# Where the S5 branch keeps its inputs and outputs, and where its six gelus are made

## The chip, the cores and the metric

One core of a Trainium2 chip runs the whole program in one launch. The metric is the device time of an execution in microseconds (us); a kernel's time is the median of its runs. The engines are named as in the profile: PE is the matmul engine (PEld its weight loads), DVE the vector engine, ACT the scalar engine, POOL the GpSimd engine, and SP the engine whose queue issues the DMAs.

## What is computed

The program is one "first block" (three branches that are gated and merged) and then two layers of a "second block", on a sequence of 512 tokens with 1024 channels. The change touches the first block alone, and there the S5 branch, a diagonal state-space model on 768 channels:

```
def first_block(x, mem, ...):
    h = rms_norm(x, g_norm)
    q, k, v, fl, gf, u, gs, qm, gm, gl = split_cols(h @ w_in)
    y_fox = forgetting_attention(q, k, v, log_sigmoid(fl + b_forget)) * silu(gf)

    y_s5 = s5_ssm(u, lam_re, lam_im, log_step, b_re, b_im, c_re, c_im, d_skip)
    y_s5 = gelu(y_s5)
    y_s5 = y_s5 * sigmoid(y_s5 @ w_glu + b_glu)
    y_s5 = y_s5 * silu(gs)

    y_mem = memory_attention(qm, mk, mv) * silu(gm)
    merged = gates[0] * (y_fox @ w_proj_fox) + gates[1] * (y_s5 @ w_proj_s5) + gates[2] * (y_mem @ w_proj_mem)
    return rms_norm(x + merged @ w_out, g_final)
```

Everything is fp32. A product of fp32 matrices is made of three matmuls on split operands: high by high, low by high, high by low.

## The kernel before

**Tiles.** Data lie in SBUF as tiles of 128 partitions by 512 fp32 values, nearly all from one ring of 85 (`u()`). A projection is made in blocks: one block is 128 output channels by 512 tokens in one PSUM bank (`pmm`, three of them), so 24 matmuls of 128x512 where there are 8 tiles of input channels, and 18 where there are 6. Two or more blocks share a strip of weights. A strip is loaded (`wr`), its high part is cast on ACT (`wh`, L93), and its low part is the difference (`wl`, L96), made on DVE or POOL. Strips are split three ahead of the one in use.

**Order.** Each engine runs its own queue in the order in which a scheduler wrote it, from the program order and its own estimates, so an instruction that waits holds up all behind it on its engine. Some long work is written as generators in the background: `tick` advances them by a rate for every block of foreground work, up to each `yield`, which names a cost. The S5 generator has rate 0.2, later 0.25; the generator that makes the second block's modulation (`ada_gen`, tiles `adw` and `adacc`, L491 to L520: each round sums eight `adw` tiles into one `adacc` on DVE) has rate 0.37 and starts in `s5_out`.

**The first block in order of time.** A head projects the six tiles of u. `upost` (L1498) copies each to SBUF, writes it to a DRAM tensor `ud[j]`, and reads it back at once in another layout (`u4`, four DMAs, L1505): channels and time are interleaved differently in the scan. Then `fox` makes the forgetting attention of six pairs of heads (scores L320, exponentials L388, products with v L409 to L411), `memory` the memory attention and its projection, and `s5_out` (L1689) finishes the S5 branch. Under `fox` and `memory` the S5 generator (`s5_gen`, L1334) works through six batches, one per tile of u.

**A batch** (`s5_batch`, L1228) makes transposes (L1258), input matmuls (L1269), a scan on DVE, small matmuls (L1313) whose result DVE copies into `s5to` (L1318), and 12 matmuls (L1322 to L1324) into `py`. DVE adds the skip term (`s5du`), four DMAs write it to DRAM (`yd[j]`, L1329), and one DMA reads it back in the order of the projections (`s5y`, L1331).

**The gelu** of a batch (`gelu`, L1675) is seven instructions on one 128x512 tile: Square on ACT (L1679), a tensor_scalar (L1084) and a product (L1087) on DVE, Tanh on ACT (L1682), (t+1)*y on DVE (L1090), the high part `yh` on ACT (L1420) and the low part `yl` on DVE (L1090). In `s5_gen` the gelu of batch j-1 comes behind batch j, for j from 1 to 5, each followed by a yield of 1.5. The yields of the six batches and the five gelus make 86.1 together.

**s5_out** projects gs in six blocks (24 matmuls each; ACT Tanh L1696, then a DVE product: tile `gst`). The last gelu stands behind the fourth of them (`GE = 4`). Then come six blocks of glu, 18 matmuls each: every one sums over all six gelu tiles, three matmuls per tile. Their results go through ACT (`glt`, L1703) and DVE; then the projection `p5`, and the output.

Of the kernel before, what the change touches and what calls it, by code (L numbers as in the profile page):

```python
# [1069 lines left out]
class Blk1(Blk2):  # L1070
# [2 lines left out]
    F0 = 12  # L1073
    NF = 4
    ZM = 0.6
    GE = 4
    RS5, RS5B, RADA = 0.2, 0.25, 0.37


# [146 lines left out]
                self.tt(d[r, :, :, g, :], t[2 * i][r], t[2 * i + 1][r], op)  # L1226
        yield 1.3

    def s5_batch(self, j, U, y):


        S = self.S5
# [33 lines left out]
        for i in range(2):  # L1266
            p = self.p("a")
# [22 lines left out]
        a, b2, c, d = (self.u(name="s5h") for _ in range(4))  # L1290
# [25 lines left out]
        for i in range(4):  # L1316
            n = 128 - 32 * i
# [9 lines left out]
        self.tt(du, du, py, ALU.add)  # L1327
        for i in range(4):
            self.nc.sync.dma_start(out=self.yd[j].rearrange("(q c) (i b) -> i c q b", q=4, i=4)[i], in_=v4(du)[32 * i:32 * i + 32])  # L1329
        y[j] = self.u(name="s5y")  # L1330
        self.nc.sync.dma_start(out=y[j], in_=self.yd[j])  # L1331
        yield 0.6

    def s5_gen(self, u, y, ge, ges):  # L1334
        for j in range(6):
            yield from self.s5_batch(j, u[j], y)
            if j > 0:
                self.gelu(j - 1, ge, ges)
                yield 1.5

    def forget_load(self):
        nc = self.nc
# [131 lines left out]
    def block1(self):  # L1474
        nc, b = self.nc, self.base
        cst = self.t(b, [128, 1], F32, "hpi")
        nc.vector.memset(cst, 1.5707963267948966)
        self.halfpi = cst
        self.bmh = self.t(b, [128, 24], F32, "bmh")
        nc.vector.tensor_scalar(out=self.bmh, in0=self.col("b_merge", 0, 24), scalar1=0.5, scalar2=None, op0=ALU.mult)  # L1480
        self.bgh = self.t(b, [128, 6], F32, "bgh")
        nc.vector.tensor_scalar(out=self.bgh, in0=self.col("b_glu", 0, 6), scalar1=0.5, scalar2=None, op0=ALU.mult)
        x = [self.u(name="x") for _ in range(8)]
        with self.tc.high_priority():
            for hf in range(2):
                for j in range(8):
                    if 8 * hf + j == self.F0:
                        self.fetch(0)
                    nc.sync.dma_start(out=self.half(x[j], hf), in_=self.half(self.a["x"][:, j, :], hf))
        for hf in range(2):  # L1490
            for j in range(8):
                self.sq_acc(self.half(x[j], hf), j, slice(256 * hf, 256 * hf + 256))
        h = self.new_h()
        norm = self.norm(x, self.col("g_norm", 0, 8), None, h)
        u = [None] * 6
        self.y5 = [None] * 6

        def upost(j):  # L1498
            def f(pm):
                t = self.u(name="us")  # L1500
                nc.scalar.copy(t.rearrange("p (i b) -> p b i", i=4), pm.rearrange("p (b i) -> p b i", i=4))
                nc.sync.dma_start(out=self.ud[j], in_=t)
                u[j] = self.u(name="u4")
                for i in range(4):
                    nc.sync.dma_start(out=u[j][32 * i:32 * i + 32].rearrange("p (q b) -> p q b", q=4),  # L1505
                                      in_=self.ud[j].rearrange("(q c) (i b) -> i c q b", q=4, i=4)[i])
            return f
        self.head(["u"] * 2, h, [upost(j) for j in range(2)],
                  norm, self.half, True)
        del x, norm  # L1510
        fl = self.forget_load()
        self.s5_load()
        self.load16()
        self.merge(self.strip("u", h, 8, [upost(j) for j in range(2, 6)]), [])
        merged = []
        ge, ges = [], ([], [])
        hm = self.fox(h, u, ge, ges, merged, fl)
        self.memory(h, hm, merged)
        return self.s5_out(h, ge, ges, merged)

    def fox(self, h, u, ge, ges, merged, fl):
        nc = self.nc
        g = self.forget(h, *fl)
        next(g)
        self.lag.append(g)
        yf = [None] * 6
        Q, K, V, FK = {}, {}, {}, {}
        blks = [slice(128 * i, 128 * i + 128) for i in range(4)]

        def f_proj(p):  # L1530
            def vev(pm, b0, nb):
                for i in range(2):
                    key = p + i
                    if b0 == 0:
                        V[key] = self.v_new()
                    self.v_put(V[key], pm[:, :, 128 * i:128 * i + 128], b0, nb)

            def put(isq):
                def f(pm):
                    self.put(pm, isq, lambda hh, t: (Q if isq else K).__setitem__(2 * p + hh, t), 0.125 if isq else None)  # L1540
                    if not isq:
                        t = self.ring.tile([128, 2, T], BF16, tag="u", name=f"fk{p}", bufs=self.NU)
                        for hh in range(2):
                            nc.scalar.activation(out=t[:, hh, :], in_=self.FK, func=AF.Copy,
                                                 scale=self.self_f[:, 2 * p + hh:2 * p + hh + 1])
                            FK[2 * p + hh] = t[:, hh, :]
                return f
            it = self.tm_items("fv", h, 256, vev) if p % 2 == 0 else []
            return it + self.strip("fqk", h, 8, [put(True), put(False)])

        def f_unit(p):
            def dst(j):
                if yf[p] is None:
                    yf[p] = self.u(name="yf")
                return yf[p]
            return self.unit(
                2,
                lambda qb: [[(0, 128 * qb + 128, "f", blks[qb], slice(0, 128 * qb + 128), (128 * qb, 128, self.mcq_))]],
                lambda: [([(128 * k, T - 128 * k, "f", slice(128 * k, T), blks[k], (128 * k, 128, self.mck_))],
                          [("f", k, slice(128 * k, T))]) for k in range(4)],  # L1560
                lambda j, g: self.pairs(Q[2 * p + j], K[2 * p + j]),
                lambda j, g, kb: self.v_get(V[p], kb, j),
                dst, extra=lambda j: (self.FQ, FK[2 * p + j]))
        units = [f_unit(p) for p in range(6)]
        self.merge(f_proj(0), [])
        self.s5_setup()
        self.s5 = self.add_bg(self.s5_gen(u, self.y5, ge, ges), self.RS5)
        self.merge(f_proj(1), units[0][0])
        G = {}
        gi = self.gate_items("gf", 6, h, G)  # L1570
        yfs = [], []
        it = self.branch_items(0, "pf", 6, h, yfs, merged)
        fill = gi + it[:4]
        for p in range(6):
            if p == self.PM:
                mem = self.mem_load()
            a = units[p][1]
            if p < 5:
                a = self.mix(a, units[p + 1][0], self.ZF)
            self.merge(a, f_proj(p + 2) if p < 4 else fill[:self.NF] if p == 4 else fill[self.NF:])  # L1580
        self.gated(G, yf, yfs)
        self.s5[2] = self.RS5B
        hm, mi = self.mem_prep(*mem)
        self.merge(self.mix(it[4:], mi, self.ZM), [])
        return hm
# [100 lines left out]
        ges[0].append(hi)  # L1686
        ges[1].append(lo)

    def s5_out(self, h, ge, ges, merged):  # L1689
        nc = self.nc  # L1690
        y5, gt = ([], []), []
        self.add_bg(self.ada_gen(0), self.RADA)

# [16 lines left out]
        it = []  # L1710
        for s in range(3):
            it += self.strip("gs", h, 8, [gs, gs])
        self.merge(it[:self.GE], [])
        self.gelu(5, ge, ges)
        self.merge(it[self.GE:], [])
        for s in range(3):
            for f in self.strip("glu", ges, 6, [glu(2 * s), glu(2 * s + 1)]):
                f()
# [69 lines left out]
        h = self.new_h()  # L1788
# [268 lines left out]
```

## Time and profile before

| | |
|---|---|
| time before, median of 3 runs | 2445.68 us (2441.32 to 2447.8) |
| profiled execution, its own time | 2442.14 us |
| span of that execution | 2440.4 us |
| PE busy | 2324.2 us, 95% |
| DVE busy | 1541.2 us, 63% |
| ACT busy | 1061.3 us, 43% |
| POOL busy | 887.8 us, 36% |
| mean granted clock of PE | 0.982 of full speed |

All times within the span count from its start. The first block takes roughly the first 830 us. The six gs blocks start at 621.28 us, the last batch of S5 and the memory projection lie just ahead of them. The clock column of a stretch is the mean of what was granted in it: 1.0 is 2.4 GHz, 0.5 is 1.2 GHz.

### The profile page before, as it was taken

To read this page: it belongs to the slowest core of one execution; us is meant where nothing else is said; L and a number is where in the kernel's file an instruction comes from. 1 tells how busy PE (TensorE), PEld (TensorE's weight loads), DVE (VectorE), ACT (ScalarE), POOL (GpSimd) and SP (SyncE) were. 2 spreads that over 40 slices of the span, in tenths; PEclk is the share of its full clock that TensorE was granted. 3 is DMA by queue.
4 is the path that set the end of the run, shared out by engine and by line. 5 is a ranking of instruction groups with operands and counts; after the bars stand their busy time and mean duration, and the time that the engine had idled before them with its cause. 6 is when DMAs were issued, how large, how long until landed. Compare 5 with 4: busy or idle time off the path is not lost.

```text
span 2440.4 us, 33141 instructions
## 1 busy us (share of the span) xinstructions
PE 2324.2 (95%) x12138; PEld 1938.6 (79%) x12138; DVE 1541.2 (63%) x2573; ACT 1061.3 (43%) x1995; POOL 887.8 (36%) x810
## 2 busy tenths in 40 slices
PE   6989989998999889999999999999999999999999
PEld 5877768876878867787888888887778788888888
DVE  7566887666899798658368684257974846422222
ACT  4355544443333435653444324343565444523432
POOL 2445446545232274236123223125531623122212
PEclk9999999999999999999999999999999999999999
DMA  4311122312676331122136563242211324223222
GB/s 154 110 44 52 57 76 93 113 52 66 227 269 236 124 97 53 52 79 86 61 122 246 207 237 112 82 136 76 69 48 54 98 74 139 70 95 113 95 87 87
DMA packets 105619, 265.35 MB, mean 109 GB/s; under 512 B 13664, under 2 KB 23408, under 8 KB 105456
## 3 DMA queue, kind: packets, MB, share of 16 engines
q1 hardware_dynamic: 104304, 261.47, 31.7%
q8 instruction: 95, 1.56, 0.3%
q10 hardware_dynamic: 1152, 1.77, 0.2%
q14 instruction: 68, 0.56, 0.1%
HBM read 244.69 MB, written 9.44 MB: 104 GB/s over the span
## 4 chain that ended last, share of the span: by engine, by line
PE 67%; DVE 9%; issue 4%; POOL 3%; ACT 2%; DMA 1%; SPq 0%; POOLq 0%; DVEq 0%; ACTq 0%
PE pmm L117 18%; PE pmm L119 18%; PE pmm L118 18%; PE ps L320 3%; DVE wl L96 1%; DVE adacc L514 1%; PE ppv L409 1%; PE ppv L411 1%; PE ppv L410 1%; DVE l L232 1%; POOL qv L632 1%; PE pmm L134 1%; PE pmm L135 1%; PE ps L629 1%; PE pmm L133 1%
## 5 line engine op out<-in xcount | busy, mean ns | idle before, releaser
L96 POOL TENSOR_TENSOR wl<-wr,wh 128x512 fp32r<-128x512 f32 x346 | 482.4, 1413 | 1149.2 <-ACT wh L93 945.0
L117 PE MATMUL pmm<-h,wh 128*128 128x512 f32 (+1 forms) x2112 | 826.0, 392 | 6.5 <-ACT wh L93 2.8
L119 PE MATMUL pmm<-h,wl 128*128 128x512 f32 (+1 forms) x2112 | 825.8, 392 | 4.5 <-POOL wl L96 4.3
L118 PE MATMUL pmm<-l,wh 128*128 128x512 f32 (+1 forms) x2112 | 823.6, 390 | 0.0
L117 PEld LDWEIGHTS pmm<-h,wh 128*128 128x128 f32 x2112 | 400.6, 190 | 86.9 <-ACT wh L93 3.8
L119 PEld LDWEIGHTS pmm<-h,wl 128*128 128x128 f32 x2112 | 400.4, 190 | 86.4 <-POOL wl L96 7.0
L118 PEld LDWEIGHTS pmm<-l,wh 128*128 128x128 f32 x2112 | 400.7, 190 | 77.7 <-DVE l L230 0.4
L93 ACT CAST wh<-wr 128x512 fp32r<-128x512 f32 (+1 forms) x692 | 385.7, 611 | 135.7 <-DMA wr<-in_w 102.2
L96 DVE TENSOR_TENSOR wl<-wr,wh 128x512 fp32r<-128x512 f32 x346 | 288.4, 863 | 27.9 <-ACT wh L93 24.0
L392 DVE TENSOR_TENSOR pl<-pe,ph 128x512 fp32r<-128x512 f32 (+4 forms) x168 | 111.9, 674 | 133.9 <-ACT ph L390 131.9
L230 DVE TENSOR_TENSOR l<-r,h 128x512 fp32r<-128x512 f32 x64 | 46.4, 725 | 220.8 <-ACT h L222 216.7
L972 DVE SCALAR_TENSOR_TENSOR x<-pmm,ada,x 128x512 f32<-128x512 f32 (+1 forms) x88 | 59.9, 682 | 179.8 <-PE pmm L119 179.4
L514 DVE SCALAR_TENSOR_TENSOR adacc<-adw,cact,adacc 128x512 f32<-128x512 f32 x168 | 156.5, 933 | 3.2
L320 PE MATMUL ps<-qk,qk 128*128 128x512 f32 (+4 forms) x416 | 140.5, 363 | 11.2 <-DVE unm L345 3.6
L995 ACT ACTIVATE r<-pmm 128x512 f32<-128x512 f32 x62 | 37.1, 598 | 257.2 <-PE pmm L119 254.7
L388 ACT ACTIVATE pe<-ps 128x512 f32<-128x512 f32 (+4 forms) x168 | 84.5, 503 | 91.3 <-PE ps L320 88.8
L320 PEld LDWEIGHTS ps<-qk,qk 128*128 128x128 f32 x416 | 79.9, 193 | 32.2 <-DVE unm L345 8.0
L117 PE MATMUL pmm<-yh,wh 128*128 128x512 f32 (+1 forms) x244 | 91.1, 376 | 5.6 <-ACT yh L1420 3.6
L632 POOL TENSOR_TENSOR qv<-qv,mhalf 128x8 f32<-128x8 f32 x34 | 60.4, 1778 | 91.0 <-DVE qv L631 86.7
L119 PE MATMUL pmm<-yh,wl 128*128 128x512 f32 (+1 forms) x244 | 90.7, 373 | 1.7 <-DVE wl L96 0.9
L390 ACT CAST ph<-pe 128x512 fp32r<-128x512 f32 (+4 forms) x168 | 88.8, 529 | 7.9 <-DVE pl L392 1.7
L118 PE MATMUL pmm<-yl,wh 128*128 128x512 f32 (+1 forms) x244 | 90.5, 372 | 0.4 <-DVE yl L1090 0.4
(386 smaller groups left out, 3992.7 us busy)
## 6 DMA issues: line engine op xcount, KB each, us to landing
wr<-in_w SPq DMA_DIRECT2D x324, 512.0 KB
adw<-in_wada SPq DMA_DIRECT2D x192, 256.0 KB
xs<-xg SPq DMA_DIRECT2D x136, 64.0 KB
wr<-in_w SPq DMA_DIRECT2D x22, 384.0 KB
xd<-x SPq DMA_DIRECT2D x16, 256.0 KB
x<-xd SPq DMA_DIRECT2D x16, 256.0 KB
x<-in_x SPq DMA_DIRECT2D x16, 128.0 KB
x<-in_x SPq DMA_DIRECT2D x8, 256.0 KB
```

Of the source, the lines that this page charges most:

```text
L93: ins = self.nc.scalar.copy(h[:, 0:m], r[:, c:c + m])
L96: eng.tensor_tensor(out=l[:, 0:m], in0=r[:, c:c + m], in1=f32(h)[:, 0:m], op=ALU.subtract)
L117: mm(out, wh, ah, start=start, stop=False)
L118: mm(out, wh, al, start=False, stop=False)
L119: self.pe = mm(out, wl, ah, start=False, stop=stop).ins.name
L320: mm(outs[i] if len(r.shape) == 2 else outs[i].rearrange("p (r i) -> p r i", r=r.shape[1]), w, r, start=first and i == 0, stop=last and i ...
L388: nc.scalar.activation(out=e[:, w], in_=pt[:, w], func=AF.Exp)
L390: nc.scalar.copy(ph[:, w], e[:, w])
L392: nc.vector.tensor_tensor(out=pl[:, w], in0=e[:, w], in1=f32(ph)[:, w], op=ALU.subtract)
L514: nc.vector.scalar_tensor_tensor(out=acc, in0=w, scalar=cc, in1=acc, op0=ALU.mult, op1=ALU.add)
L632: nc.gpsimd.tensor_tensor(out=v, in0=v, in1=self.mhalf, op=ALU.pow)
L972: nc.vector.scalar_tensor_tensor(out=x[j][:, s], in0=pm[:, s], scalar=ada[:, c + j:c + j + 1], in1=x[j][:, s], op0=ALU.mult, op1=ALU.add)
```

## The change

What it does:

- `upost` writes `ud[j]` and no longer reads it back. `s5_gen` does that: it loads batch 0 at its start, and batch j+1 just ahead of batch j's work. The same 24 DMAs now stand in SP's queue among the weight loads of the S5 stage.
- `s5_batch` writes `yd[j]` and no longer reads it back. `s5_out` issues all six reads at its start, ahead of the first `adw` loads.
- The five gelus and their yields of 1.5 leave `s5_gen`. The S5 generator is advanced at the same rates, with 78.6 of work where it had 86.1.
- `s5_out` makes all six gelus, one behind each gs block (`merge` of six blocks with six gelus). Before, five were long done and one stood behind the fourth block.

```
-        y[j] = self.u(name="s5y")
-        self.nc.sync.dma_start(out=y[j], in_=self.yd[j])
         yield 0.6
 
-    def s5_gen(self, u, y, ge, ges):
+    def s5_gen(self):
+        def load(j):
+            u = self.u(name="u4")
+            for i in range(4):
+                self.nc.sync.dma_start(out=u[32 * i:32 * i + 32].rearrange("p (q b) -> p q b", q=4),
+                                       in_=self.ud[j].rearrange("(q c) (i b) -> i c q b", q=4, i=4)[i])
+            return u
+        u = load(0)
         for j in range(6):
-            yield from self.s5_batch(j, u[j], y)
-            if j > 0:
-                self.gelu(j - 1, ge, ges)
-                yield 1.5
+            n = load(j + 1) if j < 5 else None
+            yield from self.s5_batch(j, u)
+            u = n
...
                 nc.sync.dma_start(out=self.ud[j], in_=t)
-                u[j] = self.u(name="u4")
-                for i in range(4):
-                    nc.sync.dma_start(out=u[j][32 * i:32 * i + 32].rearrange("p (q b) -> p q b", q=4),
-                                      in_=self.ud[j].rearrange("(q c) (i b) -> i c q b", q=4, i=4)[i])
...
-    def s5_out(self, h, ge, ges, merged):
+    def s5_out(self, h, merged):
         nc = self.nc
+        ge, ges = [], ([], [])
+        self.y5 = [self.u(name="s5y") for _ in range(6)]
+        for j in range(6):
+            nc.sync.dma_start(out=self.y5[j], in_=self.yd[j])
         y5, gt = ([], []), []
         self.add_bg(self.ada_gen(0), self.RADA)
...
-        self.merge(it[:self.GE], [])
-        self.gelu(5, ge, ges)
-        self.merge(it[self.GE:], [])
+        self.merge(it, [lambda j=j: self.gelu(j, ge, ges) for j in range(6)])
```

No engine gains or loses work by it but for a few scheduling rows. In the changed program the lines from L1330 on are shifted by a few, so a gelu reads L1675, L1083, L1086, L1678, L1089 and L1423 there. What the change moves is seen in the queues at three places.

**ACT in the gs stage.** `gst` is the Tanh of a gs block, `gw` the work tile of a gelu, `yh` its high part, `wh` the casts of a strip of weights. Before, from the third `gst` to the fifth:

```order
L1696 ACTIVATE gst_6206<-pmm_6181 128x512
L93 CAST wh_6220<-wr_6065 128x512
L93 CAST wh_6224<-wr_6065 128x512
L1696 ACTIVATE gst_6255<-pmm_6230 128x512
L1679 ACTIVATE gw_6267<-s5y_5876 128x512
L1682 ACTIVATE gw_6267<-gw_6267 128x512
L1420 ACTIVATE yh_6273<-gw_6267 128x512
L93 CAST wh_6277<-wr_6132 128x512
L93 CAST wh_6281<-wr_6132 128x256
L1696 ACTIVATE gst_6312<-pmm_6287 128x512
```

and now, from the third `gst` to the casts behind the fourth:

```order
L1696 ACTIVATE gst_6176<-pmm_6151 128x512
L1675 ACTIVATE gw_6190<-s5y_5997 128x512
L1678 ACTIVATE gw_6190<-gw_6190 128x512
L1423 ACTIVATE yh_6196<-gw_6190 128x512
L93 CAST wh_6200<-wr_6015 128x512
L93 CAST wh_6204<-wr_6015 128x512
L1696 ACTIVATE gst_6235<-pmm_6210 128x512
L1675 ACTIVATE gw_6247<-s5y_5998 128x512
L1678 ACTIVATE gw_6247<-gw_6247 128x512
L1423 ACTIVATE yh_6253<-gw_6247 128x512
L93 CAST wh_6257<-wr_6092 128x512
L93 CAST wh_6261<-wr_6092 128x256
```

The same six rows stand there six times over: each block's `gst` now has the whole gelu of the block ahead of it, and two casts, in front of it.

**DVE in the gs stage.** Of each gs block DVE makes the product `gst`; the rest is `adacc` sums, low parts of weights and gelu. Before, the rows about the second `gst`:

```order
L514 SCALAR_TENSOR_TENSOR adacc_6111<-adw_6103,cact_84,adacc_6111 128x512
L1090 SCALAR_TENSOR_TENSOR gst_6159<-gst_6159,pmm_6134 128x512
L514 SCALAR_TENSOR_TENSOR adacc_6111<-adw_6105,cact_84,adacc_6111 128x512
L96 TENSOR_TENSOR wl_6172<-wr_6025,wh_6171 128x512
L96 TENSOR_TENSOR wl_6176<-wr_6025,wh_6175 128x512
L514 SCALAR_TENSOR_TENSOR adacc_6111<-adw_6107,cact_84,adacc_6111 128x512
```

and now, from the end of the first gelu to the head of the third:

```order
L1089 SCALAR_TENSOR_TENSOR yl_6081<-gw_6074,yh_6080 128x512
L518 TENSOR_TENSOR adacc_6061<-adacc_6061 64x512
L1089 SCALAR_TENSOR_TENSOR gst_6119<-gst_6119,pmm_6094 128x512
L1083 TENSOR_SCALAR gw_6131<-gw_6131 128x512
L1086 TENSOR_TENSOR gw_6131<-gw_6131,s5y_5996 128x512
L1089 SCALAR_TENSOR_TENSOR gw_6131<-gw_6131,s5y_5996 128x512
L1089 SCALAR_TENSOR_TENSOR yl_6138<-gw_6131,yh_6137 128x512
L96 TENSOR_TENSOR wl_6142<-wr_5963,wh_6141 128x512
L96 TENSOR_TENSOR wl_6146<-wr_5963,wh_6145 128x512
L512 TENSOR_SCALAR adacc_6183<-adw_6062,cact_84 128x512
L1089 SCALAR_TENSOR_TENSOR gst_6176<-gst_6176,pmm_6151 128x512
```

Gelus 0, 2 and 4 have `adacc` sums between their steps, gelus 1, 3 and 5 have none. From the first `gst` to the last gelu's `yl` DVE now has 6 `gst`, 28 rows of the modulation, 4 low parts of weights and 6 gelus; before, from the first `gst` to the first glu block's product, it had 6, 26, 6 and 1.

**PE at the end of the last S5 batch.** Before, 27 matmuls of a gate projection stood between the last L1313 of batch 5 and the 12 matmuls that need `s5to`; the last three of them, and what follows:

```order
L117 MATMUL pmm_5950<-h_182,wh_5831 128x512
L118 MATMUL pmm_5950<-l_190,wh_5831 128x512
L119 MATMUL pmm_5950<-h_182,wl_5832 128x512
L1322 MATMUL ps_5856<-u_144_628,s5to_5825 128x128
L1323 MATMUL ps_5856<-s5m_5533,s5cw_5757 128x128
L1324 MATMUL ps_5856<-s5m_5535,s5cw_5758 128x128
```

and now the L1313 (L1312 in its lines) are directly ahead:

```order
L1312 MATMUL ps_5587<-s5cw_5477,s5b_1261_5581 32x128
L1312 MATMUL ps_5587<-s5cw_5478,s5b_1261_5581 32x128
L1321 MATMUL ps_5602<-u_962_4294,s5to_5596 128x128
L1322 MATMUL ps_5602<-s5m_5241,s5cw_5477 128x128
L1323 MATMUL ps_5602<-s5m_5243,s5cw_5478 128x128
```

Batch 5 itself has moved up by about 150 of PE's rows, out of the memory projection into the memory attention. At the end of `fox` it is the other way round: batch 1's L1313 and L1322 stood there with nothing between them, and now have 23 matmuls of scores, of a gate projection and of products with v in between; DVE's reciprocal for the last pair of heads (L439) stood ahead of that batch's `s5to` copies, and now stands behind them. From the first gs block on PE's queue is the same in both, but for a few neighbours swapped far behind.

## Rows read from the trace of the kernel before

**Rows 1.** The page, part 1: busy us of each engine, share, instructions.

```profile
PE 2324.2 (95%) x12138; PEld 1938.6 (79%) x12138; DVE 1541.2 (63%) x2573; ACT 1061.3 (43%) x1995; POOL 887.8 (36%) x810
```

**Rows 2.** Windows: length, busy PE, PEld, DVE, ACT, POOL; PE clock, DMA, GB/s.

```profile
100.00:621.40 521.40, 479.74 (x2582) 392.48 (x2581) 372.07 (x591) 242.65 (x466) 273.12 (x279) 0.96 0.22 72
270.00:300.00 30.00, 26.48 (x124) 20.10 (x123) 24.82 (x39) 16.55 (x31) 16.25 (x17) 0.89 0.17 52
340.00:370.00 30.00, 21.86 (x108) 18.45 (x107) 21.57 (x32) 10.52 (x19) 8.77 (x10) 0.83 0.21 66
627.55:661.80 34.25, 34.25 (x157) 28.46 (x156) 32.07 (x42) 11.37 (x21) 7.61 (x6) 1.00 0.68 235
661.80:700.00 38.20, 36.53 (x162) 29.13 (x161) 33.23 (x48) 15.70 (x30) 11.00 (x8) 1.00 0.63 217
```

**Rows 3.** Waits of PE from 100 to 621.4: total us, times, longest.

```profile
PE ps L1322 <- DVE s5to L1318: 6.0, 2, 4.7
PE ps L1313 <- DVE s5b L1309: 5.5, 3, 3.0
...
PE pmm L117 <- ACT yh L1420: 3.6, 2, 2.3
...
PE ps L320 <- ACT pe L388: 3.1, 3, 2.2
```

**Rows 4.** Timeline of PE: the first gs matmul, the first that needs gelu 5.

```profile
621.28 0.39 PE L117 MATMUL pmm<-h,wh 128*128 128x512 f32 x1
...
658.03 0.39 PE L117 MATMUL pmm<-yh,wh 128*128 128x512 f32 x1
```

**Rows 5.** Timeline of ACT: the first gs block's Tanh and two casts behind it.

```profile
626.92 0.60 ACT L1696 ACTIVATE gst<-pmm 128x512 f32<-128x512 f32 x1 [8.24 <-PE pmm L119]
627.41 1.14 ACT L93 CAST wh<-wr 128x512 fp32r<-128x512 f32 x2
```

**Rows 6.** Timeline of DVE: the first gs product, the first glu product.

```profile
627.55 0.69 DVE L1090 SCALAR_TENSOR_TENSOR gst<-gst,pmm 128x512 f32<-128x512 f32 x1 [4.66 <-ACT gst L1696]
...
661.81 0.68 DVE L1090 SCALAR_TENSOR_TENSOR gw<-glt,gw 128x512 f32<-128x512 f32 x1
```

**Rows 7.** Groups of DVE from 627.55 to 661.8: count, busy us, mean ns.

```profile
L514 DVE SCALAR_TENSOR_TENSOR adacc<-adw,cact,adacc 128x512 f32<-128x512 f32 x20 | 16.3, 813 | 0.5
...
L96 DVE TENSOR_TENSOR wl<-wr,wh 128x512 fp32r<-128x512 f32 (+1 forms) x6 | 3.3, 594 | 0.0
```

**Rows 8.** The gelu's tile: ns min/median/max of each step, first and last start.

```profile
L1679 ACT ACTIVATE gw<-s5y x6: 1085/1129/1151, 270.9 to 643.8; 128x512 f32<-128x512 f32 x6
L1084 DVE TENSOR_SCALAR gw<-gw x6: 416/418/427, 276.0 to 646.6; 128x512 f32<-128x512 f32 x6
L1087 DVE TENSOR_TENSOR gw<-gw,s5y x6: 1039/1082/1100, 276.4 to 647.6; 128x512 f32<-128x512 f32 x6
L1682 ACT ACTIVATE gw<-gw x6: 630/631/632, 277.5 to 648.7; 128x512 f32<-128x512 f32 x6
L1090 DVE SCALAR_TENSOR_TENSOR gw<-gw,s5y x6: 1036/1079/1101, 278.1 to 650.2; 128x512 f32<-128x512 f32 x6
L1420 ACT ACTIVATE yh<-gw x6: 629/632/633, 279.2 to 651.4; 128x512 fp32r<-128x512 f32 x6
L1090 DVE SCALAR_TENSOR_TENSOR yl<-gw,yh x6: 691/692/693, 279.9 to 652.0; 128x512 fp32r<-128x512 f32 x6
```

**Rows 9.** Timeline from 638 to 650 us: POOL, and two DVE sums of one form.

```profile
638.98 2.72 POOL L96 TENSOR_TENSOR wl<-wr,wh 128x512 fp32r<-128x512 f32 x2 [8.16 <-ACT wh L93]
...
640.59 1.66 DVE L518 TENSOR_TENSOR adacc<-adacc 64x512 f32<-64x512 f32 x1
...
649.37 0.69 DVE L520 TENSOR_TENSOR adacc<-adacc 64x512 f32<-64x512 f32 x1
```

**Rows 10.** Timeline about 280 us: an exponential of fox behind gelu 0.

```profile
279.22 0.63 ACT L1420 ACTIVATE yh<-gw 128x512 fp32r<-128x512 f32 x1 [1.10 <-DVE gw L1090]
279.87 0.60 ACT L388 ACTIVATE pe<-ps 128x512 f32<-128x512 f32 x1
```

More of the change, by code (lines that the diff above doesn't have):

```diff
@@ L1075 @@
     ZM = 0.6
-    GE = 4
     RS5, RS5B, RADA = 0.2, 0.25, 0.37
@@ L1227, in s5_mul, with s5_batch @@
         yield 1.3
-    def s5_batch(self, j, U, y):
+    def s5_batch(self, j, U):
         S = self.S5
@@ L1494, in block1 @@
         norm = self.norm(x, self.col("g_norm", 0, 8), None, h)
-        u = [None] * 6
-        self.y5 = [None] * 6
         def upost(j):
@@ L1515, in block1, with fox @@
         merged = []
-        ge, ges = [], ([], [])
-        hm = self.fox(h, u, ge, ges, merged, fl)
+        hm = self.fox(h, merged, fl)
         self.memory(h, hm, merged)
-        return self.s5_out(h, ge, ges, merged)
-    def fox(self, h, u, ge, ges, merged, fl):
+        return self.s5_out(h, merged)
+    def fox(self, h, merged, fl):
         nc = self.nc
@@ L1566, in fox @@
         self.s5_setup()
-        self.s5 = self.add_bg(self.s5_gen(u, self.y5, ge, ges), self.RS5)
+        self.s5 = self.add_bg(self.s5_gen(), self.RS5)
         self.merge(f_proj(1), units[0][0])
```

## The prediction

> **What bounds the kernel now.** The page's busy line comes first: PE is busy for 2324.2 us, 95% of the span, and no other engine for more than 63% [rows 1]. So the time is PE's work plus the time in which PE stands or runs at half clock, and an edit that leaves PE's matmuls alone can only change the second part. That average hides that stages have different limits, so windows come next. The S5 stage (100 to 621.4) is 521.40 us with 479.74 us of PE: 41.7 us are lost there, at a mean clock of 0.96. The stage where the gelus go is another case: from 627.55 to 661.80 PE is busy all 34.25 us, but DVE is busy for 32.07 of them, ACT for only 11.37 and POOL for 7.61 [rows 2]. DVE has 2.2 us to spare there. PE does not wait for DVE only because nothing that PE wants early stands at the end of DVE's queue.
>
> The waits tell what PE lost in the S5 stage, and the timelines where the edges of the gs stage lie; both are used below.
>
> **The edits that cost nothing by themselves.** The 24 reads of u move in SP's queue from the head of the kernel to a batch ahead of their use; the six gelus start from 270.9 to 643.8 [rows 8], so a batch lasts some 75 us, and that covers them. The six reads of `s5y` stand ahead of the `adw` loads; the first gelu cannot start before the first gs block is through ACT, 626.92 + 0.60, which is 5.6 us after that stage's first matmul [rows 4, 5]. That covers them, and if it did not, the delay would fall on the gelus priced next. The reads of batch 5 come late only if its writes do, and that batch now ends earlier than before.
>
> **The gs stage.** Five gelus are added. One costs DVE 0.418 + 1.082 + 1.079 + 0.692 = 3.27 us and ACT 1.129 + 0.631 + 0.632 = 2.39 us [rows 8]. I take the new queues row by row, from the `gst` of block 0, which starts on DVE at 627.55 as before [rows 6].
>
> DVE's content: 5 x 3.27 = 16.4 us more; two rows of the modulation more, one of them like L518's 1.66 and one of 0.81 [rows 7, 9], 2.5; two low parts of weights fewer at 0.59 [rows 7], -1.2. Against before's 34.25 us that is 34.25 + 17.7 = 52.0, less the 2.2 us that stood idle, 49.8. But not all of it can be dense. Gelus 1, 3 and 5 have no other work between their steps, and DVE waits there for Square, Tanh and `yh` on ACT: after such a `gst` 1.1 us for Square, part of it hidden, 0.63 + 0.05 for Tanh, and the same for `yh`. I take 1.3 us each, 3.9 in all: 53.7. So `yl` of gelu 5 ends near 627.55 + 53.7 = 681.2, and its `yh` 0.7 earlier, at 680.5.
>
> PE reaches the first matmul that needs gelu 5 at 658.03, 36.75 us after its first gs matmul at 621.28 [rows 4]. It is in the first of the six glu blocks, so no later glu work can go ahead of it on PE's queue. PE stands for 680.5 - 658.0 = 22.5 us, in two or three pieces (gelus 3, 4 and 5 each come later than PE wants them). The gs blocks themselves are hardly held: ACT now takes a `gst` only behind the gelu ahead of it, some 9 us apart where PE makes a block in 5.44 us, but three banks of `pmm` let PE run ahead, and what it waits there it would wait later.
>
> After a wait PE runs at half clock for a time. In the window from 270 to 300, with its waits about 280, the clock's mean is 0.89, so 30 x 0.11 = 3.3 us of full speed are missing; from 340 to 370 it is 0.83, 5.1 us for two pieces [rows 2]. One such piece after the last wait adds 3.3; pieces between the waits cost nothing, as PE is early there. Sum of the stage: +25.8.
>
> Bounds. Lower: the serial chain alone, with DVE always free. Per block ACT has `gst` 0.60, Square 1.13, then ts 0.42 and product 1.08 on DVE, Tanh 0.63, product 1.08, `yh` 0.63, and two casts 1.14 [rows 5, 8]: 6.7 us against PE's 5.44. Five times 6.7 from 626.92, then 5.57 for the last one, ends at 666.0, 8 us after 658.0; with 3.3 for the clock, +11. That would need the 28 modulation sums out of the gelus' way, and the queue puts ten to fourteen of them between steps, so I take the value near the DVE sum. Upper: each of the three pairs without cover costs 2.5 us instead of 1.3, +3.6, and the odd `adacc` waits for its load, +2: +31.
>
> One row shows a longer cost: L518, a sum of 64x512 in SBUF, took 1.66 us, most of it while POOL was at work from 638.98 to 641.70, and the same form at L520 took 0.69 [rows 9]. So an instruction of POOL can cost one of DVE's about 1.0 us. POOL has six low parts in the stage [rows 2], so up to +5.8, if each met a gelu step where it met none before. The six gelus' own steps spread little, from 1.036 to 1.101 us for the longest [rows 8], so I leave it out of the sum and keep it for the upper end. The Trainium skill (page "SBUF — State Buffer", section "Who interferes with whom") states that a DVE instruction with two SBUF inputs contends with a GpSimd instruction that reads SBUF, and that the loser blocks for the whole instruction. By that rule three of a gelu's four DVE steps can be blocked and the stage would be some +32 instead of +26; the trace agrees in L518's 1.66 us, and no gelu step in it shows it.
>
> **The S5 stage.** PE's waits that a gelu or an S5 step ends are L1322 6.0, L1313 5.5, `yh` 3.6, `pe` 3.1: 18.2 us [rows 3]. Only some of them go:
> - About 280, an exponential of fox stands on ACT behind gelu 0's `yh`, which ends at 279.85 [rows 10]; PE waits 2.2 us for it. With the gelu gone that wait goes, about 1 us of the one ahead of it, and the half-clock piece behind, 3.3 [rows 2]: -6.
> - At the end of fox PE waits 4.7 us for `s5to` (with no matmuls in between) and 2.3 for the `yh` that stood behind gelu 1 [rows 3]. Now 23 matmuls lie between L1313 and L1322, and no gelu stands ahead of `yh`. The chain from the last pair of heads remains, so I take 5 of the 7, and one of the two half-clock pieces there at 2.5: -7.
> - The last batch had its longest L1313 wait, 3.0 us [rows 3], in the memory projection. In its new place, inside the memory attention, nothing stands between L1313 and L1322; the nearest row for that is the 4.7 at the end of fox, which had a reciprocal ahead of the copies that is not there now. I take the whole 4.7 as new, with 3.3 for the clock, and the old 3.0 as gone: +5.
> - Batches 3 and 4 also move, in a stage where ACT and DVE are needed for exponentials. Nothing in the trace prices that. Bounds: all of the 18.2 and three pieces of clock vanish, about -28 for the whole stage; or the eleven us of L1322 and L1313 come twice with nothing saved, about +11. I take 0, between them.
>
> Sum: -8, from -28 to +11.
>
> **After the gs stage.** Behind the stall each engine's queue goes on as before, and the modulation is as far as it was. From 661.80 to 700 PE is busy for 36.53 of 38.20 us [rows 2], so at most 1.7 us can be made up. The second block is unchanged.
>
> **The sum.** 2442.1 + 25.8 - 8 - 1 = 2459 against the profiled execution; the median of the runs lies 3.5 above it, so about 2462.
>
> **The rivals** (2446 is the 2442.1 and the 3.5 of the sum).
> - *Faster, the S5 stage pays for all.* The 18.2 us of waits and the clock behind them vanish (-28), and the gelus cost only their serial chain (+11): 2446 - 17 = 2429. For it: these waits do name S5 steps, and one gelu in the gs stage costs PE nothing today. Against it: it needs DVE free for gelus in a stretch where it has 2.2 us of 34.25. It decides where the stage's cost falls under what the S5 stage gives back.
> - *No difference.* The gs stage is at +16, because modulation sums wait for the gelus' steps anyway and fill them, and the S5 stage gives back 16: 2446.
> - *Dearer.* Gelu steps on DVE are held up by POOL's low parts as L518 was (+32 for the stage), and the moved batches stall the memory attention for as much as they give back elsewhere (0): 2446 + 32 - 1 = 2477; with the S5 stage at its upper end of +11, 2488. For it speaks L518's row, against it the gelus' even durations. It decides where POOL works at the same time as a gelu's steps; it has the sign of the forecast.
> - *The change does not act.* The scheduler would have to leave the gelus where they were; the new queues show that it has not. No chance.
>
> **How the numbers follow.** A measurement of this kernel tells a difference from none above about 0.3%, 7.3 us. My forecast (stage +20 to +31, S5 stage -14 to 0) has 0.52, the dearer rival 0.16, no difference 0.21, faster 0.11. So slower 0.68, same 0.21, faster 0.11. The forecast's own span is about 2452 to 2477. Eight times in ten takes it from the middle of the cases without difference to the dearer rival's lower case: 2441 to 2479.
>
> **What would show it.** In the profile after: PE standing for about 22 us between the first glu block's matmuls, near 20 us of it on `yh` or `yl` of gelus 3 to 5, at granted clocks near 0.5 right after; DVE nearly full from the first `gst` to that `yl`, some 53 us where it was 34; no wait for `pe` behind a gelu about 280; `s5to` waits moved from the end of fox to the memory attention. It would be wrong if DVE shows idle time in the gs stage while PE runs through the glu blocks, or if the S5 stage as a whole changes by more than 15 us.

## The result

The changed kernel takes 2456.80 us (median of 4 runs, 2455.66 to 2458.56), the kernel before 2445.12 us beside it. The ratio is 1.0053, with a 95% interval of 1.004 to 1.0065: 11.7 us or half a per cent slower. 2462 was predicted, in a range of 2441 to 2479.

The page of the changed kernel: PE is as busy as before, and the span is longer [rows 1].

```profile
PE 2327.1 (95%) x12111; PEld 1940.2 (79%) x12138; DVE 1546.5 (63%) x2573; ACT 1061.8 (43%) x1995; POOL 886.5 (36%) x810
```

The two edges of the gs and glu stage are the Tanhs on ACT, first and last start of `gst` and `glt`:

```profile
L1696 ACT ACTIVATE gst<-pmm x6: 587/588/598, 620.3 to 664.9; 128x512 f32<-128x512 f32 x6
L1703 ACT ACTIVATE glt<-pmm,bgh x6: 678/682/689, 675.0 to 700.2; 128x512 f32<-128x512 f32 x6
```

Before, the same view gave:

```profile
L1696 ACT ACTIVATE gst<-pmm x6: 592/598/600, 626.9 to 654.1; 128x512 f32<-128x512 f32 x6
L1703 ACT ACTIVATE glt<-pmm,bgh x6: 678/682/688, 658.9 to 687.1; 128x512 f32<-128x512 f32 x6
```

So the S5 stage ends 6.6 us earlier (626.9 to 620.3), and from the first `gst` to the last `glt` it is 79.9 us where it was 60.2: 19.7 us lost. The sum is +13.1 at the last `glt`, and the first exponential of the second block (L388) comes 13.6 us later than before (946.0 against 932.4). The medians differ by 11.7. The profiled execution itself is 16.4 longer (2458.56 against 2442.14): some 3 us more lie in the second block, whose code is the same; their cause is open.

Windows of the changed kernel (columns as in [rows 2]): the S5 stage, the two windows of [rows 2] in it, and the stretch from the first `gst` product to the last gelu's `yl`.

```profile
100.00:614.60 514.60, 474.04 (x2573) 390.09 (x2581) 357.48 (x572) 231.92 (x451) 268.29 (x279) 0.97 0.24 76
...
620.90:673.90 53.00, 41.63 (x159) 31.02 (x158) 48.01 (x63) 21.60 (x35) 8.56 (x6) 0.90 0.42 145
...
270.00:300.00 30.00, 26.92 (x147) 21.13 (x147) 23.85 (x32) 18.49 (x33) 21.41 (x21) 0.94 0.23 70
340.00:370.00 30.00, 28.06 (x155) 23.51 (x154) 19.09 (x27) 13.16 (x27) 18.85 (x23) 1.00 0.27 81
```

In the 53.00 us DVE is busy for 48.01 and PE for 41.63 at a clock of 0.90; before, PE had no gap in the 34.25 us of that stretch [rows 2]. PE's timeline has the gaps one by one, in brackets:

```profile
614.63 0.39 PE L117 MATMUL pmm<-h,wh 128*128 128x512 f32 x1
...
646.56 0.50 PE L117 MATMUL pmm<-h,wh 128*128 128x512 f32 x1 [2.52 <-ACT wh L93]
...
664.24 1.14 PE L117 MATMUL pmm<-yh,wh 128*128 128x512 f32 x2 [4.60 <-DVE adacc L514]
665.18 0.63 PE L118 MATMUL pmm<-yl,wh 128*128 128x512 f32 x1
666.73 0.79 PE L118 MATMUL pmm<-yl,wh 128*128 128x512 f32 x1 [0.92 <-DVE yl L1089]
...
671.91 0.40 PE L117 MATMUL pmm<-yh,wh 128*128 128x512 f32 x1
...
673.25 1.01 PE L117 MATMUL pmm<-yh,wh 128*128 128x512 f32 x3 [0.48 <-ACT yh L1423]
```

and ACT's has what three of them waited for, the cast of a weight behind gelu 2 and `yh` of gelus 4 and 5:

```profile
645.37 0.63 ACT L1423 ACTIVATE yh<-gw 128x512 fp32r<-128x512 f32 x1 [1.76 <-DVE gw L1089]
645.90 1.12 ACT L93 CAST wh<-wr 128x512 fp32r<-128x512 f32 x2
...
663.56 0.63 ACT L1423 ACTIVATE yh<-gw 128x512 fp32r<-128x512 f32 x1 [1.76 <-DMA adw<-in_wada]
...
672.57 0.63 ACT L1423 ACTIVATE yh<-gw 128x512 fp32r<-128x512 f32 x1 [1.15 <-DVE gw L1089]
```

The 4.60 is put down to `adacc`, but the matmul reads `yh` of gelu 4, which ACT made at 663.56 for 0.63 us. The matmul of 673.25 is the one that needs gelu 5; by the distance of before (36.75 us behind the first gs matmul, [rows 4]) PE wanted it at 651.4, so it is 21.9 us late. PE's gaps up to there sum to 11.1 us: 6.0 on gelus 4 and 5 (the last three brackets), and 5.1 in and just behind the gs blocks on parts of weights, whose casts now stand behind the gelus on ACT. The rest of the 21.9 us is work. PE's matmuls started 0.43 us apart from 664.75 to 671.58, at half clock, and 0.23 apart at full clock, and the 0.48 shows that PE had work nearly until gelu 5 came. That work is the second glu block. PE's queue of the changed kernel, from the first row that reads gelu 4:

```
L117 MATMUL pmm_6386<-yh_6315,wh_6261 128x512
L117 MATMUL pmm_6429<-yh_6080,wh_6319 128x512
L118 MATMUL pmm_6429<-yl_6081,wh_6319 128x512
L118 MATMUL pmm_6386<-yl_6316,wh_6261 128x512
L119 MATMUL pmm_6386<-yh_6315,wl_6262 128x512
L119 MATMUL pmm_6429<-yh_6080,wl_6320 128x512
L117 MATMUL pmm_6429<-yh_6137,wh_6319 128x512
```

6386 is the first glu block and 6429 the second: 15 of its 18 matmuls stand ahead of the first block's rows for gelu 5. Before, all 18 rows of the first block stood ahead of the second. The text ahead of the prediction says that PE's queue is the same from the first gs block on; that is wrong at this place.

### The profile page after: what moved, and what is told of

Its sections match the earlier page's. It is cut to its first block, busy times and chain, and to the rows that moved or that the text cites. A ratio compares the mean times of both kernels' runs of the same rounds, so it can differ in the third digit from the quotient of the medians.

```text
span 2456.7 us, 33106 instructions
## 1 busy us (share of the span) xinstructions
PE 2327.1 (95%) x12111; PEld 1940.2 (79%) x12138; DVE 1546.5 (63%) x2573; ACT 1061.8 (43%) x1995; POOL 886.5 (36%) x810
## 3 DMA queue, kind: packets, MB, share of 16 engines
q10 hardware_dynamic: 1152, 1.77, 0.2%
## 4 chain that ended last, share of the span: by engine, by line
PE 63%; DVE 11%; issue 4%; POOL 3%; ACT 3%; DMA 2%; SPq 1%; POOLq 0%; DVEq 0%; ACTq 0%
PE pmm L117 17%; PE pmm L119 17%; PE pmm L118 16%; PE ps L320 4%; DVE adacc L514 1%; PE ppv L409 1%; PE ppv L411 1%; PE ppv L410 1%; DVE wl L96 1%; DMA xs<-xg 1%; POOL qv L632 1%; POOL wl L96 1%; DVE yl L1089 1%; DVE l L232 1%; DMA adw<-in_wada 1%
## 5 line engine op out<-in xcount | busy, mean ns | idle before, releaser
L118 PEld LDWEIGHTS pmm<-l,wh 128*128 128x128 f32 x2112 | 400.9, 190 | 78.6 <-DVE l L230 0.4
L96 DVE TENSOR_TENSOR wl<-wr,wh 128x512 fp32r<-128x512 f32 x346 | 282.8, 845 | 50.1 <-ACT wh L93 45.6
L388 ACT ACTIVATE pe<-ps 128x512 f32<-128x512 f32 (+4 forms) x168 | 84.5, 503 | 105.6 <-PE ps L320 102.9
L117 PE MATMUL pmm<-yh,wh 128*128 128x512 f32 (+1 forms) x244 | 91.3, 380 | 11.1 <-DVE adacc L514 4.6
```

What stands on the lines that cost most here:

```text
L96: eng.tensor_tensor(out=l[:, 0:m], in0=r[:, c:c + m], in1=f32(h)[:, 0:m], op=ALU.subtract)
L117: mm(out, wh, ah, start=start, stop=False)
L118: mm(out, wh, al, start=False, stop=False)
L388: nc.scalar.activation(out=e[:, w], in_=pt[:, w], func=AF.Exp)
```

## Experiments

The table has each kernel's median, the median of before beside it, the ratio with its interval, and the two edges. The last column is the gs and glu stage. In e4 and e11 the first `gst` stands behind a gelu on ACT, so it is no edge there.

| kernel | us | before | ratio | first gst | last glt | stage |
|---|---|---|---|---|---|---|
| before | 2445.12 | | | 626.9 | 687.1 | 60.2 |
| changed | 2456.80 | 2445.12 | 1.0053 [1.0040, 1.0065] | 620.3 | 700.2 | 79.9 |
| e1 gelus alone | 2471.78 | 2441.91 | 1.0124 [1.0109, 1.0139] | 633.7 | 713.5 | 79.8 |
| e2 DRAM alone | 2443.24 | 2441.91 | 1.0006 [0.9997, 1.0015] | 622.7 | 682.9 | 60.2 |
| e5 yields kept | 2455.92 | 2441.91 | 1.0056 [1.0041, 1.0071] | 617.5 | 697.1 | 79.6 |
| e6 no gelu arithmetic | 2435.49 | 2441.91 | 0.9973 [0.9963, 0.9982] | 618.7 | 679.2 | 60.5 |
| e3 modulation later | 2466.23 | 2443.01 | 1.0097 [1.0082, 1.0112] | 621.7 | 689.6 | 67.9 |
| e4 gelus in memory's projection | 2440.41 | 2443.01 | 0.9992 [0.9982, 1.0001] | | 680.7 | |
| e9 three gelus | 2462.92 | 2443.01 | 1.0080 [1.0063, 1.0096] | 637.2 | 703.4 | 66.2 |
| e7 e1 + u ahead | 2484.96 | 2443.01 | 1.0171 [1.0151, 1.0191] | 643.9 | 723.7 | 79.8 |
| e8 e1 + y late | 2449.02 | 2443.25 | 1.0026 [1.0015, 1.0037] | 616.3 | 696.3 | 80.0 |
| e10 y one batch later | 2473.07 | 2443.25 | 1.0121 [1.0101, 1.0141] | 635.1 | 714.3 | 79.2 |
| e11 e4 + u at once | 2434.63 | 2443.25 | 0.9961 [0.9947, 0.9975] | | 673.5 | |
| e12 ring of 79 | 2464.17 | 2444.01 | 1.0082 [1.0053, 1.0112] | 619.1 | 699.2 | 80.1 |

### The two halves of the change, and the gelu itself: e1, e2, e6

e1 is the kernel before with

```
-            if j > 0:
-                self.gelu(j - 1, ge, ges)
-                yield 1.5
...
-        self.merge(it[:self.GE], [])
-        self.gelu(5, ge, ges)
-        self.merge(it[self.GE:], [])
+        self.merge(it, [lambda j=j: self.gelu(j, ge, ges) for j in range(6)])
```

> The kernel before with the gelus alone moved behind the gs blocks; u is read back at once and y right behind its writes, as before. Theory (the loss lies in the gelus' place in the gs stage, the DRAM part is free): as the changed kernel, 2457 us within 3, first gs matmul at 614 to 616 us, first glt 60 us behind it. Rival (late reads of u or y are part of the loss): under 2452 us.

e2 is the kernel before with the other half:

```
-                u[j] = self.u(name="u4")
...
-        y[j] = self.u(name="s5y")
-        self.nc.sync.dma_start(out=y[j], in_=self.yd[j])
         yield 0.6
...
+            n = load(j + 1) if j < 5 else None
+            if j > 0:
+                self.yload(j - 1)
             yield from self.s5_batch(j, t, y)
```

> The kernel before with the DRAM part alone: u read one batch ahead, y read one batch later, gelus and their yields where they were. Theory: no difference from before, 2445 us within 4. Rival (the reads cost, behind weight loads in SP's queue): 2450 us or more.

e6 is the changed kernel with the first seven lines of `gelu`, its arithmetic, left out:

```
-        nc.scalar.activation(out=w3, in_=y, func=AF.Square)
...
-        self.stt(w3, w3, 1.0, y, ALU.add, ALU.mult)
+        w = self.y5[j]
```

> The changed kernel with the gelu's arithmetic left out: of each gelu only yh and yl remain, made from y itself, so ACT loses 1.76 us and DVE 2.58 us per gelu. Theory (the chain of the gelus through ACT and DVE is the loss): the stall before the first glu block falls under 3 us, the S5 stage keeps its 6.7 us, 2437 to 2440 us. Rival (the loss is the wait for the reads of y, or the order of ACT's queue as such): 2450 us or more.

The stage column answers one question at once: 79.8 with the gelus moved and nothing else, 60.2 with the DRAM half alone, 60.5 with the moved gelus' arithmetic left out. The 19.7 us are the moved gelus' steps in that stage, wholly: in e6 PE waits there for 1.5 us in all, for parts of weights alone, so the reads of y and the places of `yh` and `yl` on the queues cost nothing by themselves. e6 takes 2435.49 us, a little under the expected range. e2 as a whole cannot be told from before, as expected. But e1 missed by 15 us: its stage is as expected, and its S5 stage ends 13.4 us later than the changed kernel's. So with late gelus the DRAM half is not free there; it gains. That was against the theory, and e7, e8, e10 and e12 go into it below.

### What sets the end of gelu 5: e9, e3

e9 makes three gelus behind their batches again (their y is read at the start of the next batch):

```
             yield from self.s5_batch(j, u)
             u = n
+            if 0 < j < 4:
+                self.gelu(j - 1, *self.gg)
...
-        self.merge(it, [lambda j=j: self.gelu(j, ge, ges) for j in range(6)])
+        self.merge(it, [lambda j=j: self.gelu(j, ge, ges) for j in range(3, 6)])
```

> The changed kernel with gelus 0 to 2 made behind their batches again and gelus 3 to 5 in the gs stage, behind every second block. Theory (each gelu adds its 3.27 us to a DVE that has 2 us to spare): DVE's way from the first gst to the last gelu's yl is 53 - 3 x 3.3 = 43 us or a little less, PE loses 8 to 11 us before the second glu block, where it lost 20. Rival (what costs is that the last gelu stands behind the sixth block, however many there are): PE loses 18 us or more, as with six.

Its window from the first `gst` product to the last gelu's `yl` (columns as in [rows 2]), and PE's one large wait in the glu blocks:

```profile
637.90:676.80 38.90, 35.74 (x159) 29.01 (x157) 37.38 (x51) 15.06 (x26) 7.98 (x6) 0.98 0.53 183
```

```profile
675.30 1.41 PE L117 MATMUL pmm<-yh,wh 128*128 128x512 f32 x3 [3.16 <-DVE adacc L514]
```

38.90 us with three gelus, 53.00 with six: 4.7 us for each, 3.5 of them DVE's work (37.38 and 48.01 us busy) and 1.2 its waits, which stand between the steps of gelus 1, 3 and 5 of the changed kernel. The stage loses 66.2 - 60.2 = 6.0 us where six lose 19.7. The rival falls: in e9, too, the last gelu stands behind the sixth block. The expected 43 us and 8 to 11 us of loss were too much; a gelu costs more than its DVE steps. As a whole e9 takes 2462.92 us, more than the changed kernel, since its S5 stage ends at 637.2; that belongs to the next part.

e3 takes the modulation out from between the gelus:

```
-        self.add_bg(self.ada_gen(0), self.RADA)
...
         self.merge(it, [lambda j=j: self.gelu(j, ge, ges) for j in range(6)])
+        self.add_bg(self.ada_gen(0), self.RADA)
```

> The changed kernel with the modulation's generator started behind the gs blocks and not ahead of them, so that no adacc sum stands between the gelus. Theory (DVE's content, gelus plus modulation, sets when gelu 5 is done): only the serial chain through ACT and DVE remains, so the first glt comes 40 to 43 us after the first gst on ACT (54.7 in the changed kernel), PE loses about 8 us there and not 20; but the 28 sums, 22 us, must then lie behind, where DVE is 92% busy, so the whole is 2448 to 2458 us. Rival (the lockstep on ACT alone sets it): first glt still 52 to 55 us behind the first gst.

The first `glt` comes 41.0 us behind the first `gst` (662.7 and 621.7), so the chain alone is what is left, and the stage loses 7.7 us where the lower bound of the prediction had 8 before the clock. The sums on DVE between the gelus make the other 12. Up to 3 of these may be POOL's: without the sums none of the six `yl` meets POOL's work, and each takes 0.69 us, where three took 1.8 in the changed kernel. But the sums do not vanish. PE's waits of e3 from 690 to 880 us (us in total, times, longest), and the window 780 to 860 of e3 and then of before:

```profile
PE pmm L119 <- DVE wl L96: 6.1, 1, 6.1
PE ps L491 <- DVE adacc L520: 5.2, 1, 5.2
```

```profile
780.00:860.00 80.00, 58.70 (x361) 53.72 (x360) 63.78 (x115) 26.63 (x55) 17.18 (x12) 0.85 0.50 175
```

```profile
780.00:860.00 80.00, 67.18 (x459) 60.88 (x457) 66.94 (x120) 30.87 (x62) 23.61 (x17) 0.97 0.38 128
```

PE stands at the end of the block instead, for a low part of a weight that DVE made behind sums, and for the modulation itself, at a clock of 0.85, and the whole is 2466: 8 us above the expected upper end, since the sums come all at the one place where the norm needs them.

### The S5 stage: e7, e8, e10, e5, e12

e7 and e8 complete a square with e1 and the changed kernel, all four with late gelus:

| first gst | y read behind its writes | y read at the end |
|---|---|---|
| u read back at once | 633.7 (e1) | 616.3 (e8) |
| u read one batch ahead | 643.9 (e7) | 620.3 (changed) |

```
+            n = load(j + 1) if j < 5 else None
             yield from self.s5_batch(j, t, y)
```

> As e1 (gelus alone moved), with u read one batch ahead in addition; y is still read behind its writes. e1 was at 2472 us, the changed kernel at 2457; e1's first gst on ACT stood at 633.7 us, that of the changed kernel at 620.3. Theory A (the place of u's reads makes the 13 us between them): first gst at 619 to 623 us, 2456 to 2460 us. Theory B (the late read of y makes them): first gst at 631 us or later, 2468 us or more.

```
-        y[j] = self.u(name="s5y")
-        self.nc.sync.dma_start(out=y[j], in_=self.yd[j])
         yield 0.6
...
+        self.y5 = [self.u(name="s5y") for _ in range(6)]
+        for j in range(6):
+            nc.sync.dma_start(out=self.y5[j], in_=self.yd[j])
```

> As e1 (gelus alone moved), with the six reads of y moved to the end of the S5 stage in addition; u is read back at once. It fills the square of u at once or ahead and y at once or late, with late gelus: e1 had its first gst at 633.7 us, e7 at 643.9, the changed kernel at 620.3. Theory (the read of y behind its writes is what costs e1 and e7 their time, and the early reads of u cost nothing): first gst at 612 to 621 us, 2450 to 2458 us. Rival (only both together help): first gst at 630 us or later, 2466 us or more.

e7 (2484.96 us) comes as its theory B, e8 (2449.02 us) as its theory. The late reads of y give back 17.4 or 23.6 us; reading u one batch ahead costs 10.2 or 4.0. The cost of u has a place. The changed kernel's PE at 117 us:

```profile
117.16 0.61 PE L277 MATMUL ps<-c,mcm 128*128 128x128 bf16 x4 [4.22 <-DVE mcm L271]
```

and that of before:

```profile
116.08 0.40 PE L277 MATMUL ps<-c,mcm 128*128 128x128 bf16 x4
```

It waits for the last of DVE's steps there, in the changed kernel and in that of before:

```profile
116.13 0.97 DVE L271 CAST mcm<-sp 128x16 bf16<-128x16 f32 x1
```

```profile
115.06 0.57 DVE L271 CAST mcm<-sp 128x16 bf16<-128x16 f32 x1
```

That result comes 1.5 us later now, and that is the smaller part. Before, PE makes 29 more matmuls of a projection while it is on its way; with u read ahead L277 stands in front of them, and PE waits for 4.2 us, and its clock is 0.67 from 117 to 125 us, where it was 1.00. Fox's first exponential comes 7 to 8 us later than before in the changed kernel, e2, e7 and e10, which read u ahead, and 0.3 or less in e1 and e8.

For y, two causes could be meant: SP's queue stands at the read until the writes have landed, or the tiles lie in the ring. e10 has the tiles but not the stand:

```
+            if j > 0:
+                self.yload(j - 1)
             yield from self.s5_batch(j, u)
...
```

> The changed kernel with the read of y of batch j not at the end but at the start of the next batch, so SP does not stand for its writes to land, but the tiles of y lie in the ring as early as in e7. Theory A (SP's queue standing between the writes and the read costs e7 its 23 us): first gst at 618 to 624 us, 2454 to 2461 us. Theory B (the tiles held in the ring cost it): first gst at 638 us or later, 2474 us or more. Theory C (neither; each small edit throws the scheduler's order of the S5 stage another way): anything between.

e12 has six tiles fewer, and nothing else:

```
-    NU = 85
+    NU = 79
```

> The changed kernel with 79 tiles in the ring and not 85, as if six tiles were held all through; PE's queue is the same row for row. Theory (early reads of y cost their time by the order of the queues, not by the tiles that they hold): first gst at 618 to 623 us, 2455 to 2461 us, as the changed kernel. Rival (held tiles delay the loads of weights, as e10 seemed to allow): first gst at 628 us or later, 2465 us or more.

e10 stays at 635.1, between its theories A and B, and e12 at 619.1: neither the stand alone (643.9 to 635.1 by taking it away, not to 620) nor the held tiles. (e12 loses its 7 us against the changed kernel behind the last `glt`, which is at 699.2; PE's queue is the same in both through the first block, but in the second, where the ring is smaller too, it is not.) What e1, e7 and e10 share, and the changed kernel and e8 have not, is an order. DVE's timeline at the end of `fox` in e10, and PE's wait for it:

```profile
363.95 3.35 DVE L439 RECIPROCAL rs<-rs 128x512 f32<-128x512 f32 x1
367.22 0.10 DVE L208 TENSOR_SCALAR nv<-ps 128x2 f32<-128x2 f32 x1
```

```profile
PE ps L197 <- POOL nr L210: 5.4, 1, 5.4
```

and DVE in the changed kernel, where PE does not wait for `nr`:

```profile
365.29 0.15 DVE L208 TENSOR_SCALAR nv<-ps 128x2 f32<-128x2 f32 x1
365.36 3.34 DVE L439 RECIPROCAL rs<-rs 128x512 f32<-128x512 f32 x1
```

A 0.1 us step stands behind a 3.3 us reciprocal, and PE behind both. e9, which reads three of the six y early, has this order too, with a wait of 5.8 us. So early reads of y go with this order in all four kernels that have them with late gelus. That it comes from the reads is argued from these four and not shown: no run changes the order alone, and the 5.4 us are one of several places that make the 14.8 between e10 and the changed kernel. That part of the cause is open.

e5 keeps the yields, so the S5 batches stand on PE's queue where they stood before:

```
             u = n
+            if j > 0:
+                yield 1.5
```

> The changed kernel with the yield of 1.5 behind each batch kept, so that the S5 batches stand on PE's queue where they stood before, but without gelus between. Theory A (the 6.7 us that the S5 stage gave back come from the gelus being gone from ACT and DVE): first gs matmul at 614 to 617 us, 2457 us. Theory B (they come from the batches' new places): first gs matmul at 619 to 622 us, 2461 to 2464 us.

Its first `gst` is at 617.5, so theory B falls: 2.8 us ahead of the changed kernel's, and it was 3.7 us ahead at L277 already, so the batches' new places give 1 us at most. e5 and e2 differ in the gelus, and in when y is read: 617.5 against 622.7, and 3 of these 5 us arise ahead of 60 us, where the two have the same edits. That leaves 2 us or so for the gelus' absence where y is read late. Where y is read early it is the other way: e1 and before, and e10 and e2, differ in the gelus and their yields alone, and the first `gst` comes 6.8 us (633.7 against 626.9) and 12.4 us (635.1 against 622.7) later without the gelus. So the runs show no gain of the gelus' absence apart from the order that comes with it.

### A place where the gelus are hidden: e4, e11

```
-        self.merge(it[4:], [])
         self.drain(self.s5)
...
+        for j in range(6):
+            nc.sync.dma_start(out=self.y5[j], in_=self.yd[j])
+        self.merge(it[4:], [lambda j=j: self.gelu(j, self.ge, self.ges) for j in range(6)])
```

> The changed kernel with the six reads of y and the six gelus moved one stage forward, between the last 12 blocks of the memory projection, behind a drain of the S5 generator. DVE is busy there for 13.8 of 34.6 us in the changed kernel. Theory (a gelu costs nothing where DVE has room for its 3.27 us): the gs and glu stage is as in the kernel before (60 us from the first gst to the last glt), what the S5 stage gave back stays, 2435 to 2441 us. Rival (gelus between projection blocks delay PE wherever they stand, by ACT's and DVE's order): 2447 us or more.

The end of the memory projection, e4 from 580 to 612 and the changed kernel from 580 to 614.6:

```profile
580.00:612.00 32.00, 32.00 (x143) 26.50 (x142) 24.25 (x31) 17.34 (x27) 8.54 (x6) 1.00 0.24 83
```

```profile
580.00:614.60 34.60, 34.60 (x154) 28.67 (x153) 13.80 (x21) 9.99 (x18) 8.14 (x6) 1.00 0.39 134
```

DVE goes from 13.80 to 24.25 us, ACT from 9.99 to 17.34, and PE has no gap in either. The same six gelus that cost 19.7 us one stage further on cost 3 us or less here (e4's last `glt` is at 680.7; that of e6, which leaves the gelus' arithmetic out, is at 679.2). e4 is 16 us faster than the changed kernel and cannot be told from before. e11 is e4 with u read back at once:

> e4 (gelus between the blocks of the memory projection, 2440 us) with u read back at once as in the kernel before, so that the new wait of 4.2 us at 117 us is gone. If the S5 stage otherwise stays as in e4: 2432 to 2437 us, faster than before by more than the uncertainty. If its order is thrown another way: 2440 us or more.

2434.63 us, 8.6 us faster than before and 22 faster than the changed kernel: the wait at 117 us is gone, and the gelus are hidden.

## Why the prediction was right, and where not

The direction and its main mechanism held: the gelus' chain through DVE in the gs stage. The numbers step by step:

- **DVE's way through the stage**: 53.7 us predicted, 53.00 measured. That it is so close is in part luck, as two parts of it missed and cancel. Three `yl` took 1.8 us and not 0.69, each while POOL made low parts: +3.3. The three L512 took 0.48 and not about 1.4, since POOL did not work beside them: -2.9. DVE in the changed kernel (POOL's 3.03 us run from 646.58):

```profile
621.50 0.48 DVE L512 TENSOR_SCALAR adacc<-adw,cact 128x512 f32<-128x512 f32 x1
...
646.70 1.77 DVE L1089 SCALAR_TENSOR_TENSOR yl<-gw,yh 128x512 fp32r<-128x512 f32 x1
```

and one L512 of before, beside POOL's work from 638.98 [rows 9]:

```profile
639.03 1.52 DVE L512 TENSOR_SCALAR adacc<-adw,cact 128x512 f32<-128x512 f32 x1
```

- **When PE gets gelu 5**: 22.5 us late predicted, 21.9 measured.
- **What PE loses by it**: 25.8 predicted with 3.3 of half clock, 19.7 measured. This is the step that failed, in its sentence that no later glu work can go ahead on PE's queue. 15 matmuls of the second block do, 15 x 0.23 = 3.4 us of work; and as PE made them at 664 to 672 us, the half clock fell there and was over when gelu 5 came (0.40 us for the matmul of 671.91), so the 3.3 behind it did not come. The two together are 6.7 us, and the forecast was 6.1 too high. The sign that was named, near 20 us of PE standing on `yh` or `yl` of gelus 3 to 5, did not show either: it was 6.0 us, on gelus 4 and 5.
- **The S5 stage**: -8 predicted, -6.6 measured, but not by its parts. The gelus' absence gives about 2 us with y read late (e5 against e2) and costs 7 to 12 with y read early (e1, e10), where a gain of 13 was summed; the 5 us for the last batch's new place are not there (e5). The window from 340 to 370 did gain as predicted, 21.86 to 28.06 us of PE at a clock of 1.00 after 0.83 [rows 2]; but e1, which has no gelu there either, waits 5.8 us for `nr` at that place. The gain hangs on the order of the queue, not on the gelu.
- **The edits at no cost**: wrong with late gelus. The transfers are hidden, as the text says, and in the changed kernel no wait of PE in the S5 stage is put down to a DMA; what the edits cost and gave there (+4 to +10 for u, -17 to -24 for y) goes with the order that the scheduler then wrote. With the gelus left early the two edits together leave the time as it was (e2, where y is read one batch later). The S5 stage is +6.8 with the gelus' move alone (e1) and 13.4 less with the DRAM half on top; that the sum, -6.6, is near the predicted -8 is luck.
- **Rivals**: POOL's blocking, the ground of the dearer one, is there (three `yl`), but L512 gave as much back. The serial chain alone, the lower bound of +11 and the ground of the faster rival, is what e3 shows: 7.7 us.

The Trainium skill (page "SBUF — State Buffer", section "Who interferes with whom") states that a DVE instruction with two SBUF inputs contends with a GpSimd instruction that reads SBUF, and that a `tensor_scalar` can in a 2-port mode. Both agree with these traces: `yl` took 1.77 us beside POOL and 0.69 alone, L512 1.52 beside POOL and 0.48 alone.

## What to carry to other kernels

A step off the critical path is free only as far as the stage in which it stands has room on its engine: the same six gelus cost 19.7 us where DVE had 2 of 34 us free, and 3 or less where it had 21 of 35. So read the busy time of each engine by stage before moving work, and move it to the stage with room. Where a scheduler writes the queues, compare the new queues row by row at each place on which a term rests, since edits whose transfers were hidden moved the end of one stage by up to 24 us, and the queues were what differed.

## What the runs showed of the hardware

An L512 on a 128x512 tile takes 0.48 us with POOL idle, and 1.52 us at 639.03 in the kernel before, with POOL at work from 638.98 [rows 9]; that this first product of a sum is three times as fast beside an idle POOL was not expected. PE made 15 matmuls of the second block between its waits for gelus 4 and 5, most of them at half clock, and still waited 0.48 us for gelu 5: the half clock behind the first of these waits cost next to nothing there, since PE's next operand was not ready anyway.
